# A hybrid attention and MLP layer in split float32: GpSimd's work cut into pieces of 256 columns, the MLP's norm factor moved around the MLP, one gate filled in earlier, and h of two blocks kept on chip

## The chip, the cores and the metric

The kernel runs on one core of a Trainium2 chip. A core has five engines that run side by side, each with its own queue of instructions: TensorE (PE in the profile; PEld is its loading of weights), VectorE (DVE), ScalarE (ACT), GpSimd (POOL) and SyncE (SP), whose queue issues nearly all DMA transfers here. Work tiles live in the on-chip buffer SBUF (128 partitions), matmul results in PSUM, and everything else in the chip's main memory. The metric is the time of one execution in microseconds (us). The kernel before takes 3313.28 us, the median of 3 runs between 3307.74 and 3317.84.

## The reference

One step of a one-layer streaming encoder for 2048 prompt positions and 32 sample positions, all in float32, with model width 1024. Cut to what matters:

```
a  = rmsnorm(h, g_attn);  q, k, v of both groups = a @ w_in
oa = differential attention (4 heads, two maps each);  ob = chunk-band attention (8 heads of 64)
h  = h + concat(rmsnorm(oa), rmsnorm(ob)) @ w_out
c  = rmsnorm(h, g_mlp)              # h * rsqrt(mean(h*h) + eps) * g_mlp
h  = h + square(relu(c @ w_up)) @ w_down          # 1024 -> 4096 -> 1024
h  = h + sigmoid(h @ w_ple_gate) * (p @ w_ple_proj)
y  = rmsnorm(h, g_final)
```

The new keys and values of both groups are outputs as well. What matters for the change: the norm's factor r' = rsqrt(v), with v = mean(h*h) + eps, is one number per position, and relu squared takes a positive factor out as its square, so relu((h g r') W)^2 = relu((h g) W)^2 * r'^2, with r'^2 = 1/v.

## The kernel before

**Tiling.** The 2080 positions are the moving side of the matmuls, in four blocks of 512, 512, 512 and 544 columns (`BN`); the last is worked in two parts of 272 (`SUBS`). Features lie on the 128 partitions, eight rows of 128 for the width of 1024. Blocks go in halves, (0, 1) and (2, 3).

**Split float32.** Each operand is split into a high part (rounded to the format that TensorE reads) and a low part, the remainder. `split` (L146 to L153) does it: the high part on ACT (L149) or VectorE (L151), the low part, raw minus high, at L153 on GpSimd or VectorE. `mm3` (L164 to L170) makes a product out of three matmuls: high x high (L168), low x high (L169) and high x low (L170). `wunit` (L155 to L162) brings one weight unit of 512 KB: a DMA on SP's queue into `wr` (2 buffers), ACT makes `wh`, GpSimd makes `wl` (3 buffers each), in a single instruction over 1024 columns:

```
hi = self.wp.tile([P] + shape, F32R, tag="wh", bufs=3, name="wh")
lo = self.wp.tile([P] + shape, F32R, tag="wl", bufs=3, name="wl")
self.split(hi, lo, raw, hi_eng, lo_eng)
```

Such a unit feeds 24 matmuls per block: 8 rows x 3.

**Stages, in the order of the program.** The norm and projection of blocks 0 and 1 with the tables of the attention biases; differential attention over the first pairs of query tiles, with the projections to the other group beside it; band attention; projection of blocks 2 and 3; the norm of the band group's output for blocks 0 and 1 (`onorm`, its sums at L795 on GpSimd); differential attention over the other pairs (scores at L545, L559 and L582 for the weights e, L617 for the transposes); output projection of blocks 0 and 1 (`outproj`, L819 to L846); MLP of block 0, MLP of block 1; gate and final norm of block 1; output projection of blocks 2 and 3; gate of block 0; MLP of blocks 2 and 3 together, with the final norm of block 0 inside; gates and final norms of blocks 2 and 3.

**Around the change.** `outproj` adds the residual on VectorE (L838), squares on ACT, sums the squares on GpSimd (L844) and stores h in main memory (`hS`). `colnorm2` turns the sums into the norm's factor with two matmuls of ones, three ACT and four VectorE steps, and stores it (`rS`). `cnorm` (L847 to L862) then reads h and the factor back, row by row, multiplies by factor and g_mlp on VectorE (L859), and splits the result into cH and cL; odd rows' cL go to VectorE, even ones to GpSimd. The MLP goes over 16 chunks of 256 hidden features: `mlp_up` (L895 to L915) makes ups on TensorE, relu (L914) and square (L915) and the high part on ACT, the low part ul on GpSimd; `mlp_down` (L919 to L949) of the chunk before follows, and VectorE adds its result dps to h (L949). h is loaded into one tile per block ahead of the MLP. The gate (L966 to L1015) splits h, multiplies by w_ple_gate (gps), and works out sigmoid on ACT, VectorE (L994, L1012) and GpSimd (L997, L1014). The final norm (`final`, L1017 to L1071) transposes h on TensorE (yp) and stores y.

**What sets the order.** A planner orders each engine's instructions by simulating the engines in time, with the program's order as the priority; work of a later step moves ahead where its inputs and buffers are there. Buffers of one tag are handed out in the program's order, and space in SBUF and PSUM is taken over from whatever held it before, once that has been released. So a step that comes first in the program takes its weight buffers, PSUM banks and result tiles ahead of a step that comes later. `weave` and `weave2` interleave the pieces of two program steps by hand.

## Time and profile before

| | |
|---|---|
| median of 3 runs | 3313.28 us (3307.74 to 3317.84) |
| profiled execution | 3310.69 us, span 3308.8 us |
| mean TensorE clock granted | 0.975 of full speed |
| TensorE busy | 3096.1 us (94%), 17881 matmuls |
| VectorE busy | 1669.4 us (50%), 3952 instructions |
| ScalarE busy | 1698.4 us (51%), 3717 instructions |
| GpSimd busy | 1468.8 us (44%), 1083 instructions |
| DMA | 488.93 MB, 148 GB/s on average |

The span is the profiled stretch, from the first instruction to the last; 1.9 us of the execution's time lie outside of it. Busy time is the sum over an engine's instructions; the profile's page also gives it in 40 equal slices, a digit for tenths. A group of the profile is all instructions of one line, engine and shape: its lines read "line engine operation output<-inputs shapes xcount | busy us, mean ns | idle time of the engine ahead of them, with what ended it". A wait line names the instruction that waited, what it was released by, the total in us, how many times, and the longest. A window line gives, for a stretch from A to B us, its length, the busy time of each engine with the number of its instructions, the granted TensorE clock, the share of busy DMA engines and GB/s. A timeline line gives the start in us, the duration, and in brackets how long the engine was idle before it and what released it. Matmuls overlap in the pipeline, so that a matmul's duration is longer than the distance to the next one.

### The profile page before, as it was taken

Reading aid. Unit: us, or ns where it says so; the run is one execution under the profiler, and the core shown is the slowest. Engines: PE = TensorE matmul, PEld = TensorE weight load, DVE = VectorE, ACT = ScalarE, POOL = GpSimd, SP = SyncE. Lnnn points to the kernel's source line nnn. Section 1 sums busy time; section 2 is a strip of 40 time slices with the busy share of each in tenths; the row PEclk is TensorE's granted clock in tenths of the full one; section 3 lists DMA queues with packets and bytes.
Section 4 is the critical chain, followed back from the end, with each engine's and each line's share of the span. In section 5 each row is a group of like instructions: output and inputs, shape, how many; then the busy total and the mean of one; then the engine's idle time right before and its main releaser. Section 6 shows DMA issues by size and latency. Waiting matters only on the chain. (4 is left out here: it accounts for less than half of the span.)

```text
span 3308.8 us, 50118 instructions
## 1 busy us (share of the span) xinstructions
PE 3096.1 (94%) x17881; PEld 2710.5 (82%) x17881; DVE 1669.4 (50%) x3952; ACT 1698.4 (51%) x3717; POOL 1468.8 (44%) x1083
## 2 busy tenths in 40 slices
PE   6988989999989999999899999989889999999998
PEld 6877778889977888777777877877779999999987
DVE  6117777454555545476765656656442232223335
ACT  4226666566665766666665656654442222222245
POOL 4335654432334433444544444565753333333365
PEclk9999899999999999999999999999999999999999
DMA  7488777686788654545655345347631111111123
GB/s 232 159 252 244 205 217 205 204 247 195 215 235 215 180 145 134 155 132 138 200 136 136 112 132 144 116 146 226 178 105 52 45 46 50 46 45 45 53 86 101
DMA packets 519073, 488.93 MB, mean 148 GB/s; under 512 B 37884, under 2 KB 414016, under 8 KB 518824
## 3 DMA queue, kind: packets, MB, share of 16 engines
q1 hardware_dynamic: 518824, 485.73, 50.8%
q8 instruction: 142, 2.33, 0.3%
q14 instruction: 107, 0.88, 0.1%
HBM read 379.06 MB, written 110.49 MB: 148 GB/s over the span
## 5 line engine op out<-in xcount | busy, mean ns | idle before, releaser
L153 POOL TENSOR_TENSOR wl<-wr,wh 128x1024 fp32r<-128x1024 f32 x338 | 820.0, 2427 | 1026.3 <-ACT wh L149 983.4
L949 DVE TENSOR_TENSOR h<-h,dps 128x512 f32<-128x512 f32 (+1 forms) x640 | 373.1, 585 | 584.6 <-PE dps L170 572.2
L149 ACT ACTIVATE wh<-wr 128x1024 fp32r<-128x1024 f32 x338 | 356.9, 1056 | 563.9 <-PE dps L169 278.4
L168 PE MATMUL dps<-uh,wh 128*128 128x512 f32 (+1 forms) x1280 | 459.7, 359 | 22.0 <-DVE h L949 16.7
L168 PE MATMUL ups<-cH,wh 128*128 128x512 f32 (+1 forms) x1280 | 452.0, 353 | 8.2 <-ACT relu L914 8.0
L170 PE MATMUL dps<-uh,wl 128*128 128x512 f32 (+1 forms) x1280 | 451.7, 353 | 0.0
L169 PE MATMUL ups<-cL,wh 128*128 128x512 f32 (+1 forms) x1280 | 451.5, 353 | 0.0
L169 PE MATMUL dps<-ul,wh 128*128 128x512 f32 (+1 forms) x1280 | 451.4, 353 | 0.0
L170 PE MATMUL ups<-cH,wl 128*128 128x512 f32 (+1 forms) x1280 | 451.0, 352 | 0.0
L168 PEld LDWEIGHTS dps<-uh,wh 128*128 128x128 f32 x1280 | 242.8, 190 | 57.0 <-DVE h L949 22.8
L168 PEld LDWEIGHTS ups<-cH,wh 128*128 128x128 f32 x1280 | 241.4, 189 | 40.9 <-ACT relu L914 8.6
L170 PEld LDWEIGHTS dps<-uh,wl 128*128 128x128 f32 x1280 | 241.7, 189 | 33.0
L169 PEld LDWEIGHTS ups<-cL,wh 128*128 128x128 f32 x1280 | 241.9, 189 | 31.1 <-DVE cL L153 0.4
L170 PEld LDWEIGHTS ups<-cH,wl 128*128 128x128 f32 x1280 | 241.7, 189 | 30.1
L153 POOL TENSOR_TENSOR ul<-relu,uh 128x272 fp32r<-128x272 f32 (+1 forms) x160 | 174.9, 1093 | 205.2 <-ACT uh L149 203.8
L169 PEld LDWEIGHTS dps<-ul,wh 128*128 128x128 f32 x1280 | 242.4, 189 | 26.3
L168 PE MATMUL qps<-aH,wh 128*128 128x512 f32 (+1 forms) x640 | 231.5, 362 | 6.8 <-ACT wh L149 3.4
L545 PE MATMUL s<-ka,q 128*128 128x256 f32 (+4 forms) x784 | 192.7, 348 | 40.8 <-issue 15.7
L169 PE MATMUL qps<-aL,wh 128*128 128x512 f32 (+1 forms) x640 | 229.8, 359 | 0.0
L170 PE MATMUL qps<-aH,wl 128*128 128x512 f32 (+1 forms) x640 | 229.3, 358 | 0.0
L559 ACT ACTIVATE e<-s,nm 128x512 f32<-128x512 f32 (+3 forms) x256 | 155.1, 610 | 94.7 <-DVE nm L551 70.9
L545 PEld LDWEIGHTS s<-ka,q 128*128 128x128 f32 (+1 forms) x784 | 135.7, 195 | 66.4 <-issue 27.9
(217 smaller groups left out, 7056.9 us busy)
## 6 DMA issues: line engine op xcount, KB each, us to landing
wr<-w_up SPq DMA_DIRECT2D x96, 512.0 KB, 4.2
wr<-w_down SPq DMA_DIRECT2D x96, 512.0 KB, 3.7
wr<-w_in SPq DMA_DIRECT2D x74, 512.0 KB, 5.2
q<-qS SPq DMA_DIRECT2D x256, 128.0 KB, 4.3
v<-vSa SPq DMA_DIRECT2D x64, 512.0 KB, 3.8
ka<-kS SPq DMA_DIRECT2D x32, 512.0 KB, 7.9
wr<-w_out SPq DMA_DIRECT2D x32, 512.0 KB, 5.0
wr<-w_ple_gate SPq DMA_DIRECT2D x32, 512.0 KB, 4.4
```

The lines of the kernel that those rows point to most:

```text
L149: nc.scalar.activation(hi, raw, AF.Copy)
L153: eng.tensor_tensor(lo, raw, hi.bitcast(F32), op=ALU.subtract)
L168: nc.tensor.matmul(ps, lh, rh, start=start and i == 0, stop=False)
L169: nc.tensor.matmul(ps, lh, rl, start=False, stop=False)
L170: nc.tensor.matmul(ps, ll, rh, start=False, stop=stop and i == n - 1)
L545: nc.tensor.matmul(s, q[:, m, hl, P * qi : P * qi + nr], kt[:, m, k0 : k0 + n], start=hl == 0, stop=hl == 1)
L559: nc.scalar.activation(dst, src, AF.Exp, bias=nmx, accum_out=z[:nr, m, bi : bi + 1])
L949: nc.vector.tensor_tensor(hv, hv, ps, op=ALU.add)
```

## The change

Four things change together; which products TensorE computes does not.

1. GpSimd's two-input instructions are cut into pieces of at most 256 columns (`PW = 256`, `pool_tt`): the low parts of weights (four pieces of 256 in place of one of 1024) and of activations, the sums of squares at L795 and L844, and two steps of the gate (L997, L1014).
2. The MLP's norm factor is no longer applied to its input. The input is h g_mlp, split directly out of h (`split_g`: one ACT copy with the scale g_mlp, one VectorE step for the low part). `msnorm` makes v and r = 1/v and stores both. In `mlp`, after the first chunk's `mlp_up`, GpSimd multiplies h by v, a whole block's row at a time; in the last `mlp_down`, each row, after its last addition, is multiplied by r on VectorE, or for odd rows on GpSimd where the MLP has a single block. So (h v + sum) r = h + sum / v.
3. The gate of block 0, and its final norm, come behind the MLP of block 1 and ahead of the gate of block 1, with the loading of block 2's output-projection operands woven in; they used to come behind the output projection of blocks 2 and 3. Pools for small work tiles (`wk`, `fk`) are opened once, early, and not a second time.
4. h of blocks 2 and 3 is written by their output projections directly into the tiles that the MLP uses (`hb`), and not stored and loaded again; block 2's split is made inside its output projection, block 3's behind its own. The norm of block 3 (`msnorm(3)`) moves behind the first chunk of the MLP.

```diff
 ONQ = (8, 1, 1)
+PW = 256
...
+    def pool_tt(self, out, a, b, op):
+        nc = self.nc
+        if len(out.shape) == 2:
+            n = out.shape[1]
+            m = -(-n // PW)
+            for i in range(m):
+                sl = slice(n * i // m, n * (i + 1) // m)
+                nc.gpsimd.tensor_tensor(out[:, sl], a[:, sl], b[:, sl], op=op)
+            return
+        k, n = out.shape[1:]
+        if n > PW:
+            for i in range(k):
+                self.pool_tt(out[:, i], a[:, i], b[:, i], op)
+            return
+        s = PW // n
+        for i in range(0, k, s):
+            sl = slice(i, min(i + s, k))
+            nc.gpsimd.tensor_tensor(out[:, sl], a[:, sl], b[:, sl], op=op)
+
...
             nc.vector.tensor_copy(hi, raw)
-        eng = nc.gpsimd if lo_eng == "pool" else nc.vector
-        eng.tensor_tensor(lo, raw, hi.bitcast(F32), op=ALU.subtract)
+        if lo_eng == "pool":
+            self.pool_tt(lo, raw, hi.bitcast(F32), ALU.subtract)
+        else:
+            nc.vector.tensor_tensor(lo, raw, hi.bitcast(F32), op=ALU.subtract)
...
         self.kS = self.dram([8, 2, P, KC], F32, "kS")
-        self.vS = [self.dram([KC, D], F32, "vSa"), self.dram([KC, D], F32, "vSb")]
+        self.vS = [self.dram([KC, D], F32, "vSa"), self.dram([KC, D], F32, "vSb"), self.dram([P, T], F32, "vSm")]
...
                 nc.scalar.activation(raw, raw, AF.Square)
-                nc.gpsimd.tensor_tensor(sq, sq, raw, op=ALU.add)
+                self.pool_tt(sq, sq, raw, ALU.add)
...
-    def outproj(self, b, wk, oact, ps, acc):
+    def split_g(self, k, src, n, c):
+        nc = self.nc
+        g = self.g_mlp[:, k : k + 1]
+        hi, lo = c[0][:, k, :n], c[1][:, k, :n]
+        nc.scalar.activation(hi, src, AF.Copy, scale=g)
+        nc.vector.scalar_tensor_tensor(lo, src, g, hi.bitcast(F32), op0=ALU.mult, op1=ALU.subtract)
+
+    def outproj(self, b, wk, oact, ps, acc, hfull=None, c=None):
...
             wh, wl = self.wunit(W[:, P * d : P * d + P].rearrange("(k p) c -> p k c", p=P), [8, P])
-            h = wk.tile([P, BLK], F32, tag="tmp", bufs=4, name="hd")[:, :n]
+            if hfull is None:
+                h = wk.tile([P, BLK], F32, tag="tmp", bufs=4, name="hd")[:, :n]
+            else:
+                h = hfull[:, d, :n]
...
                 nc.scalar.activation(tmp, h, AF.Square)
-                nc.gpsimd.tensor_tensor(sq, sq, tmp, op=ALU.add)
-            self.dma(self.hS[:, d, t0 : t0 + n], h)
+                self.pool_tt(sq, sq, tmp, ALU.add)
+            if hfull is None:
+                self.dma(self.hS[:, d, t0 : t0 + n], h)
+            if c is not None:
+                self.split_g(d, h, n, c)
...
-    def cnorm(self, b, wk, act, out):
-        nc = self.nc
+    def csplit(self, b, wk, act, out, hfull=None):
...
         out[b] = (cH, cL)
-        r = wk.tile([P, BLK], F32, tag="r", bufs=2, name="rl")[:, :n]
-        self.dma(r, self.rS[:, t0 : t0 + n])
         for k in range(8):
-            tmp = wk.tile([P, BLK], F32, tag="tmp", bufs=4, name="tmp")[:, :n]
-            self.dma(tmp, self.hS[:, k, t0 : t0 + n])
-            nc.vector.scalar_tensor_tensor(
-                tmp, tmp, self.g_mlp[:, k : k + 1], r, op0=ALU.mult, op1=ALU.mult
-            )
-            self.split(cH[:, k, :n], cL[:, k, :n], tmp, "act", "dve" if k % 2 else "pool")
+            if hfull is None:
+                tmp = wk.tile([P, BLK], F32, tag="tmp", bufs=4, name="tmp")[:, :n]
+                self.dma(tmp, self.hS[:, k, t0 : t0 + n])
+            else:
+                tmp = hfull[:, k, :n]
+            self.split_g(k, tmp, n, (cH, cL))
...
-    def colnorm(self, *args):
-        out = []
-        drain(self.colnorm2(*args, out))
-        return out[0]
+    def msnorm(self, sq, b, wk, ps):
+        nc = self.nc
+        n, t0 = BN[b], 512 * b
+        sh = wk.tile([P, BLK], F32R, tag="sh", bufs=1, name="msh")[:, :n]
+        sl = wk.tile([P, BLK], F32R, tag="sl", bufs=1, name="msl")[:, :n]
+        self.split(sh, sl, sq, "act", "dve")
+        r = wk.tile([P, BLK], F32, tag="r", bufs=2, name="mr")[:, :n]
+        w = wk.tile([P, BLK], F32, tag="tmp", bufs=4, name="mw")[:, :n]
+        for s0, sn in SUBS[b]:
+            ss = ps.tile([P, 512], F32, tag="mm", name="mss")[:, :sn]
+            nc.tensor.matmul(ss, self.ones, sh[:, s0 : s0 + sn], start=True, stop=False)
+            nc.tensor.matmul(ss, self.ones, sl[:, s0 : s0 + sn], start=False, stop=True)
+            v = sq[:, s0 : s0 + sn]
+            y = r[:, s0 : s0 + sn]
+            z = w[:, s0 : s0 + sn]
+            nc.scalar.activation(v, ss, AF.Copy, scale=1.0 / D, bias=EPS)
+            nc.scalar.activation(y, v, AF.Ln)
+            nc.scalar.activation(y, y, AF.Exp, scale=-1.0)
+            nc.vector.tensor_tensor(z, v, y, op=ALU.mult)
+            nc.vector.tensor_scalar(z, z, -1.0, 2.0, op0=ALU.mult, op1=ALU.add)
+            nc.vector.tensor_tensor(y, y, z, op=ALU.mult)
+        self.dma(self.vS[2][:, t0 : t0 + n], sq)
+        self.dma(self.rS[:, t0 : t0 + n], r)
...
-    def mlp_down(self, ch, nf, blocks, us, st, wk, mm):
+    def hscale(self, blocks, st, wk, src, name):
+        out = {}
+        for b in blocks:
+            out[b] = wk.tile([P, BLK], F32, tag="r", bufs=2, name=name)
+            self.dma(out[b][:, : BN[b]], src[:, 512 * b : 512 * b + BN[b]])
+        return out
+
+    def mlp_down(self, ch, nf, blocks, us, st, wk, mm, rt=None):
...
                         nc.vector.tensor_tensor(hv, hv, ps, op=ALU.add)
+                        if rt is not None:
+                            eng = nc.gpsimd if dd % 2 and len(blocks) == 1 else nc.vector
+                            eng.tensor_tensor(hv, hv, rt[b][:, s0 : s0 + sn], op=ALU.mult)
     def mlp(self, blocks, st, wk, up, mm, md):
+        nc = self.nc
...
             yield
-            if prev is not None:
+            if prev is None:
+                vt = self.hscale(blocks, st, wk, self.vS[2], "vt")
+                for d in range(8):
+                    for b in blocks:
+                        hv = st[b][0][:, d, : BN[b]]
+                        nc.gpsimd.tensor_tensor(hv, hv, vt[b][:, : BN[b]], op=ALU.mult)
+            else:
...
             prev = us
-        self.mlp_down(ch, nf, blocks, prev, st, wk, md)
+        self.mlp_down(ch, nf, blocks, prev, st, wk, md, self.hscale(blocks, st, wk, self.rS, "rt"))
...
                     nc.scalar.activation(sg, sg, AF.Ln, bias=1.0)
-                    nc.gpsimd.tensor_tensor(sg, sm, sg, op=ALU.subtract)
+                    self.pool_tt(sg, sm, sg, ALU.subtract)
...
                     hv = h[:, d, s0 : s0 + sn]
-                    nc.gpsimd.tensor_tensor(hv, hv, sg, op=ALU.add)
+                    self.pool_tt(hv, hv, sg, ALU.add)
...
             self.small = False
+            wk = opened(top, "wk", 1)
+            fk = opened(top, "fk", 1)
...
                     self.attn_a(js, pool, ps_s, ps_t, ps_o)
-            wk = opened(sq_, "wk", 1)
-            fk = opened(sq_, "fk", 1)
             self.gfin(fk)
-            acc, cn, st = {}, {}, {}
+            cn, st = {}, {}
+            acc = {b: [] for b in range(4)}
+
             def norms(b, act, ps):
-                self.colnorm(acc[b][0], b, 1.0 / D, wk, ps, "mm", self.rS)
+                self.msnorm(acc[b][0], b, wk, ps)
                 yield
-                yield from self.cnorm(b, wk, act, cn)
-
-            acc = {b: [] for b in range(4)}
+                yield from self.csplit(b, wk, act, cn)
+
...
             up = Sized(opened(top, "uh", 16, side="right"), BLK)
-            oxs = ExitStack()
-            ox = opened(oxs, "ox", 1, side="right")
-
...
                 if b == 1:
-                    drain(self.cnorm(1, wk, actq, cn))
-                    drain(self.oload(2, ox, up, oa))
-                    oxs.close()
+                    drain(self.csplit(1, wk, actq, cn))
...
                     next(m)
-                    self.colnorm(acc[1][0], 1, 1.0 / D, wk, mm, "mm", self.rS)
+                    self.msnorm(acc[1][0], 1, wk, mm)
...
                     self.dma(self.hS[:, :, 512 * b : 512 * b + 512], h)
-            drain(self.gate(1, h, uq, actq, mm))
+            with ExitStack() as x:
+                g0 = Sized(opened(x, "g0", 2, side="right"), 512, True)
+                g0h = opened(x, "g0h", 1, side="right")
+                h0 = hload(g0h, 512, 0)
+                weave(self.gate(0, h0, uq, g0, mm), self.oload(2, wk, up, oa), 1)
+                drain(self.gate(1, h, uq, actq, mm))
+                drain(self.final(0, h0, uq, fk, mm))
...
             psx.close()
-            wk = opened(top, "wk4", 1)
-            fk = opened(top, "fk4", 1)
-            self.gfin(fk)
...
             hh = opened(top, "hh", 2, side="right")
-            weave(self.outproj(2, wk, oa[2], md, acc[2]), self.oload(3, wk, act, oa), 1, 0, OW)
-            g = self.outproj(3, wk, oa[3], md, acc[3])
+            hb = {b: hh.tile([P, 8, BLK], F32, tag="h", name="h") for b in HALVES[1]}
+            g = self.oload(3, wk, act, oa)
             next(g)
-            self.colnorm(acc[2][0], 2, 1.0 / D, wk, mm, "mm", self.rS)
+            cn[2] = [act.tile([P, 8, BLK], F32R, tag="act", name=n) for n in ("cH2", "cL2")]
+            weave(self.outproj(2, wk, oa[2], md, acc[2], hb[2], cn[2]), g, 1, 0, OW)
+            g = self.outproj(3, wk, oa[3], md, acc[3], hb[3])
+            next(g)
+            self.msnorm(acc[2][0], 2, wk, mm)
             drain(g)
-            h = hload(hh, BLK, 0)
-            g = self.gate(0, h, up, act, md)
-            next(g)
-            self.colnorm(acc[3][0], 3, 1.0 / D, wk, mm, "mm", self.rS)
-            drain(g)
-            for b in HALVES[1]:
-                drain(self.cnorm(b, wk, act, cn))
-            f = self.final(0, h, up, fk, mm)
-            st = {b: (hload(hh, BLK, b),) + cn[b] for b in HALVES[1]}
+            drain(self.csplit(3, wk, act, cn, hb[3]))
+            st = {b: (hb[b],) + tuple(cn[b]) for b in HALVES[1]}
...
             next(m)
-            drain(f)
+            self.msnorm(acc[3][0], 3, wk, mm)
...
```

## The prediction

> **What bounds the kernel now.** I read the page's busy table and slices, then the stages by window, the groups by shape, what TensorE waits for, and the timeline. The page:
>
> ```profile
> PE 3096.1 (94%) x17881; PEld 2710.5 (82%) x17881; DVE 1669.4 (50%) x3952; ACT 1698.4 (51%) x3717; POOL 1468.8 (44%) x1083
> PE   6988989999989999999899999989889999999998
> POOL 4335654432334433444544444565753333333365
> ```
>
> TensorE is busy 94% of the span; nothing else passes 51%. The change leaves the matmuls as they are, so it can win only TensorE's idle time and the time of matmuls at half rate after a gap, and lose only by new idle time. The stages (projection; attention 0 and projection of blocks 2, 3; attention 1 with output projections and MLPs of blocks 0, 1; change of stage; MLP of blocks 2, 3; last gates):
>
> ```profile
> core 0: us, PE busy (x) PEld busy (x) DVE busy (x) ACT busy (x) POOL busy (x), PEclk, DMA share, GB/s
> 0.00:650.00 650.00, 567.30 (x3433) 501.05 (x3433) 358.51 (x963) 321.04 (x841) 318.32 (x273) 0.94 0.73 214
> 650.00:1350.00 700.00, 669.12 (x4030) 590.05 (x4030) 366.96 (x1175) 453.08 (x928) 252.61 (x199) 0.98 0.68 192
> 1350.00:2150.00 800.00, 752.44 (x3796) 630.57 (x3796) 514.75 (x1088) 498.27 (x1162) 371.63 (x268) 0.99 0.52 142
> 2150.00:2460.00 310.00, 275.27 (x1446) 233.18 (x1445) 169.25 (x234) 147.91 (x275) 196.85 (x119) 0.96 0.53 165
> 2460.00:3150.00 690.00, 690.00 (x4290) 626.87 (x4289) 190.09 (x367) 194.41 (x334) 230.80 (x152) 1.00 0.17 52
> 3150.00:3309.00 159.00, 141.97 (x893) 128.75 (x891) 69.80 (x129) 83.66 (x178) 98.56 (x73) 0.96 0.29 91
> ```
>
> Length less PE busy is TensorE's idle time: 82.7, 30.9, 47.6, 34.7, 0 and 17.0 us. Length times (1 - PEclk) is about the time lost to the lower clock: 39, 14, 8, 12.4, 0 and 6.4 us. The fifth stage has nothing to win.
>
> **1. The GpSimd pieces.** Groups by shape (mean ns after the comma):
>
> ```profile
> L153 POOL TENSOR_TENSOR wl<-wr,wh 128x1024 fp32r<-128x1024 f32 x338 | 820.0, 2427 | 1026.3 <-ACT wh L149 983.4 <-ACT rsy L178 11.4 <-ACT pH L624 9.7
> L153 POOL TENSOR_TENSOR vhl<-vraw,vhl 128x256 fp32r<-128x256 f32 x64 | 48.0, 750 | 92.1 <-DVE vhl L151 74.6 <-DVE stb L713 8.6 <-DVE nm L557 3.8
> L582 DVE SCALAR_TENSOR_TENSOR e<-e,c 128x256 f32<-128x256 f32 x68 | 53.0, 785 | 1.3 <-ACT e L581 1.2
> L949 DVE TENSOR_TENSOR h<-h,dps 128x512 f32<-128x512 f32 x384 | 261.9, 683 | 535.9 <-PE dps L170 534.1
> ```
>
> The biggest GpSimd group is 338 instructions of 2.43 us. What they do to VectorE is seen in the timeline (start, us, engine):
>
> ```profile
> 68.83 0.64 DVE L151 CAST vhl<-vraw 128x256 fp32r<-128x256 f32 x1
> 69.28 2.44 POOL L153 TENSOR_TENSOR wl<-wr,wh 128x1024 fp32r<-128x1024 f32 x1
> ...
> 1515.38 2.38 POOL L153 TENSOR_TENSOR wl<-wr,wh 128x1024 fp32r<-128x1024 f32 x1 [1.28 <-ACT wh L149]
> 1515.62 2.17 DVE L572 TENSOR_SCALAR c<-c,rz 128x4 f32<-128x4 f32 x1
> ```
>
> A VectorE instruction of four columns (228 ns alone) takes 2.17 us and ends at 1517.79, the GpSimd one at 1517.76. At 68.83 a cast (289 ns alone) ran until the GpSimd piece before it was over (69.32), and wl came after it. L582 at 256 columns is 476 ns where no GpSimd instruction overlaps and 1131 where one does, while h<-h,dps, one of whose inputs is in PSUM, is 682 and 683: the two exclude one another on some operands in SBUF. Summing over all VectorE instructions the time above the unhindered duration of their form gives 251 us in 238 instructions: 98, 26, 68, 51, 0 and 9 us by stage. A wait lasts until the end of the GpSimd instruction that runs; with pieces of about 0.70 us (back-to-back 256-column ones start 696 ns apart in 71 pairs) in place of 2.36 us (155 pairs), a wait should shrink to 0.3 of itself, if VectorE gets in between two pieces. Where a second GpSimd instruction was queued right behind the first, VectorE came in at the first boundary 93 times and later 6 times. So it gets in.
>
> How much of this is on TensorE's path? Its waits (total us, times, longest):
>
> ```profile
> PE rp L311 <- DVE rsy L182: 20.9, 7, 10.9
> PE dps L168 <- DVE h L949: 16.7, 14, 3.1
> PE sb L704 <- DVE stb L707: 15.7, 14, 4.4
> PE tpp L617 <- DVE e L582: 7.5, 8, 2.3
> ```
>
> VectorE ended 74.8 us of TensorE's idle time before 2150 (38.4, 16.8, 19.6 in the first three stages). All of it, with the half-clock time behind it (28), would be -103; if what it waits for is late for other reasons, 0. Removing 0.7 of the 192 us of excess in these stages is 134 us of VectorE time, more than the 74.8; the chains are long without it too, and I take 0.58 of the 74.8, **-43**, past the middle since the chains that TensorE names are where the excess sits.
>
> What the pieces cost: every further piece adds a fixed part. A weight unit goes from 2362 to 4 x 696 = 2784 ns, +0.42 us, x338 = 143; 512 columns (1255 ns) become two at 1392, +0.14; 272 (728) two of 136, +0.14 (between the 209 ns of 32 columns and the 696 of 256); 544 three, +0.27. By stage this is +35, 37, 48, 27, 38 and 16, together 200 us; with part 3 and without the cL that go to VectorE, GpSimd comes to about 1690 us, 51%. A weight unit costs GpSimd 2.78 us and TensorE 24 matmuls of 0.23 = 5.5 us with three units in flight; that cover is gone where splits of activations queue between. I cost it at 0 before 2150; it is rival D. Late next are DMA (ka<-kS 11.0 us of TensorE's waits) and issue (15.7 at L545), which stay.
>
> The Trainium skill ("SBUF — State Buffer", section "Who interferes with whom") says that VectorE and GpSimd share one port pair under an exclusive lock, held for the whole instruction, and that "Issue order, not op shape, decides who blocks". The traces agree (2.17 us for four columns). Read strictly, queued pieces would hold VectorE as long as before, which is rival B.
>
> **2. The change of stage, 2150 to 2460.** Before, gate 1 (2154 to 2229), output projections 2 and 3 (to 2339), gate 0 (to 2406), then norms of blocks 2, 3 and the MLP. TensorE idles 34.7 us there (ACT ends 19.2, VectorE 13.0 of it) and loses 12.4 to the clock, 47 together. The dearest gap is at 2413:
>
> ```profile
> 2413.32 0.30 PE L168 MATMUL ups<-cH,wh 128*128 128x272 f32 x1
> 2421.63 0.59 PE L168 MATMUL ups<-cH,wh 128*128 128x272 f32 x1 [8.01 <-ACT relu L914]
> ```
>
> After 8.0 us of idling the same matmul takes 0.59, not 0.30, until 2426; that gap and its half rate cost 10 us. It comes from norm and split of blocks 2, 3 in a row: 4 MB read back (10.5 us per block of 2 MB), 16 of L859 and 8 cL on VectorE (medians 1.03 and 1.12) and 8 cL on GpSimd. After the change block 2 is split while its output projection runs and block 3 right after it, from the tile on chip: per 128 columns one ACT copy (0.63) and one VectorE operation (0.74 at least, L859), 8 x 0.74 = 6 us for block 3. The norm's own chain (copy, Ln, Exp, three VectorE steps) leaves the path: the first up chunk doesn't need it. Removed on the SP queue: 16 stores of h, 16 loads of it, and the two r loads; added: v and r stores and loads, eight of 0.25 MB.
>
> What takes its place: gate 0 now comes first after MLP 1, ahead of gate 1, and shares its PSUM tiles, weight and result buffers in program order; its split activations need space that attention 1 still holds. TensorE leaves MLP 1 at 2152.7, the last scores are out at 2149.7, the last transposes at 2183.2, attention's last VectorE step at 2208.6. Gate 1 filled that time. Left alone with TensorE, the rest of attention (30 us to its transposes, now interleaved with gate 1) should shrink to about 10; if it doesn't, 20 more, and the -20 below is 0. Then two gates in a row: one of 512 columns has 55.2 us of matmuls and 48.7 of GpSimd, after the change 55.7, so GpSimd leads by little: I take 6 us over both, 4 for finals, 4 for block 3's split, which waits for the output projection's operands to free their buffers, 3 for part 3. 10 + 6 + 4 + 4 + 3 = 27 against 47: **-20** (ends: all of 47 kept beside the hole, +11; only the 7.5 us of waits on weights left, -40).
>
> **3. The norm factor around the MLP.** Added: 8 multiplications of h by v per block on GpSimd, unsplit, 24 x 1.255 + 8 x 1.329 = 41 us, queued behind the first up chunk and ahead of the next chunk's weight splits. For blocks 2, 3 that is 21 us in one go; a chunk takes TensorE 690 / 16 = 43 us for four units, and three units are ahead, about 22 us of cover: the 3 us above. And the last mlp_down multiplies each result by r. In single-block MLPs half goes to GpSimd, hidden (0). For blocks 2, 3 per 128 rows: VectorE 683 + 2 x 438 and the same three again from SBUF, 2.69 with 0.74 for the first, against TensorE's 2.75: no slack, and GpSimd excludes it: **+5** (0 to +12).
>
> **4. Gates 2 and 3.** Alone at the end, 115 us of matmuls, GpSimd 48.7 + 54.5 = 103 before, 118 after: it becomes the longer. **+5** (0 to +15).
>
> **Sum.** Against the profiled execution of 3310.7 (span 3308.8 and 1.9 around it; 2.6 below the median of 3313.28): -43 - 20 + 5 + 5 = -53, so 3310.7 - 53 = **3258** us.
>
> **Rivals.** B: VectorE gains nothing. For: queued pieces may pass the lock on (against: 93 to 6), and the rsqrt chains (20.9) wait on ACT too. Only -10 is left: 3301. C: the reorder opens a wide hole: gate 0 waits until attention's last store (2222) leaving TensorE idle for 60 us, 50 more than taken: 3308. For: TensorE's tiles and the planner's slots go in order; against: the last transposes are long done by then.
>
> The Trainium skill ("TensorE: Matmul & The Clock Gate", Part 1) has the rate halve after an idle window of about 3.4 us; the row at 2421 agrees (0.59 after 8.0 us), and a hole of 60 us would add by it only some 3 us.
>
> D, slower: GpSimd becomes the bound where it is busiest. In the first, fourth and last stage it is busy 49, 63 and 62%, and the pieces add 35 + 27 + 16 = 78 us there; each lo part comes 0.42 us later. It takes the whole gain from where 53 of the 78 (68%) reach TensorE; if all do: 3258 + 78 = 3336. Against it: GpSimd sat idle 1026 us ahead of the weight splits.
>
> **How the numbers follow.** My forecast 0.53, B 0.14, C 0.08, D 0.25. The likeliest's own range is 3215 (part 1 at -75, part 2 at -31) to 3300 (part 1 at -15, part 2 at -6). The range for 8 in 10 runs from 3205 to 3338, which takes in B and C and most of D. Less than 0.3% (10 us) from the median can't be told from no change; B lies at that bound (3303) and goes half to each side: faster 0.53 + 0.07 = 0.60, same 0.07 + 0.08 = 0.15, slower 0.25.
>
> **What the profile after would show.** wl as 1352 instructions of about 0.70 us and POOL near 1690 us busy; L582 at 256 columns near 500 instead of 785 ns; TensorE's idle time before 2150 at about 118 instead of 161; no gap of 8 us ahead of ups for blocks 2, 3; gate 0's first matmul some 10 us behind MLP 1's last. The forecast is wrong if VectorE's durations fall and TensorE's idle time doesn't (late for another reason), if TensorE's waits name GpSimd's wl or ul at all often (D), or if gate 0 starts 30 us or more behind MLP 1 (C).

## The result, and the profile after

The changed kernel takes 3331.1 us (median of 8 runs, 3321.6 to 3340.0) against 3313.2 us (8 runs): a ratio of 1.0058, interval 1.0038 to 1.0077. It is slower by 0.6%, where 1.7% faster was forecast. A second measurement beside the experiments gave 1.0054 (1.0037 to 1.0070). Its profiled execution took 3321.6 us (span 3319.6), 9.5 below its median, so what is read from one trace below is put beside ratios of medians.

The page of the changed kernel, busy time by engine and TensorE's and GpSimd's slices:

```profile
PE 3104.0 (94%) x17881; PEld 2706.6 (82%) x17881; DVE 1556.1 (47%) x3963; ACT 1702.0 (51%) x3717; POOL 1728.6 (52%) x2519
PE   7988999899889999999999999868899999999998
POOL 5436776332345544655744545557584334333387
```

VectorE is 113 us less busy and GpSimd 260 us more, much as forecast (1690 us; the pieces take 0.76 us on average, not 0.70). TensorE has a new low, 8 and 6, in slices 26 and 27. The stages by window show the same. Each kernel's change of stage is cut here from the last matmul of MLP 1 to the first down matmul of blocks 2 and 3, so the cuts lie elsewhere for each. Before:

```profile
1350.00:2152.00 802.00, 754.44 (x3805) 632.20 (x3805) 516.65 (x1093) 499.09 (x1163) 373.63 (x269) 0.99 0.52 142
2152.00:2441.00 289.00, 255.28 (x1333) 216.24 (x1331) 153.62 (x192) 138.49 (x243) 191.74 (x116) 0.95 0.54 168
3165.00:3309.00 144.00, 126.97 (x798) 115.00 (x797) 57.23 (x108) 76.30 (x167) 89.08 (x67) 0.96 0.31 97
```

After (the change of stage in three parts):

```profile
0.00:650.00 650.00, 584.36 (x3609) 516.84 (x3609) 326.77 (x1019) 340.35 (x894) 371.03 (x542) 0.96 0.76 225
650.00:1350.00 700.00, 663.41 (x3924) 579.55 (x3924) 331.39 (x1122) 437.30 (x888) 288.75 (x448) 0.98 0.67 190
1350.00:2133.00 783.00, 745.58 (x3733) 622.93 (x3734) 491.21 (x1080) 495.96 (x1146) 441.87 (x606) 0.98 0.50 141
2133.00:2180.00 47.00, 17.45 (x90) 14.33 (x88) 22.46 (x46) 17.88 (x43) 18.79 (x27) 0.65 0.36 120
2180.00:2320.00 140.00, 121.92 (x488) 93.09 (x489) 32.12 (x42) 60.69 (x92) 101.80 (x141) 0.97 0.27 82
2320.00:2459.00 139.00, 126.28 (x783) 113.84 (x781) 72.49 (x131) 70.53 (x140) 88.78 (x126) 0.95 0.47 152
3180.00:3320.00 140.00, 125.19 (x792) 112.93 (x792) 63.57 (x121) 76.90 (x170) 110.05 (x173) 0.95 0.31 100
```

By the end of MLP 1 the changed kernel is 19 us ahead (2133 against 2152). Then it needs 326 us where 289 were needed before, and so the lead is lost with 18 us more; from there on it gains back 7 (720.6 us for the MLP of blocks 2, 3 against 724.3, since block 0's final norm has gone out of it, and 140 for the end against 144). The loss has a place: the 47 us from 2133 to 2180, with 17.45 us of matmuls and a granted clock of 0.65. The timeline of that place:

```profile
2132.83 0.39 PE L192 MATMUL dps<-uh,wl 128*128 128x512 f32 x1
2140.57 1.12 PE L639 MATMUL tpp<-ident,e 128*128 128x128 f32 x4 [7.20 <-DVE e L604]
2166.62 0.39 PE L665 MATMUL ss<-sl,ones_r 128*128 128x32 f32 x1
2170.24 0.25 DVE L667 SCALAR_TENSOR_TENSOR os<-os,g_sub_s,rsy 128x32 f32<-128x32 f32 x1 [1.98 <-POOL rsy L204]
2170.52 0.32 SPq L145 DMA_DIRECT2D oT<-os  x1
2170.89 0.56 SPq L145 DMA_DIRECT2D h<-hS  x1
2179.38 2.19 ACT L169 ACTIVATE hH<-h 128x512 fp32r<-128x512 f32 x4 [8.14 <-DMA h<-hS]
2180.07 0.79 PE L190 MATMUL gps<-hH,wh 128*128 128x512 f32 x1 [13.05 <-ACT hH L169]
```

MLP 1 ends at 2132.8. The rest of attention, alone on TensorE, still takes until 2167, a chain of small steps over four engines. Its last step on VectorE ends at 2170.5, and its last store (oT) goes out behind that. The load of block 0's h stands right behind this store in SyncE's queue: it goes out at 2170.9, lands 8 us later, is split on ACT, and gate 0 starts at 2180.1. The load fills space that attention held, but by the addresses in the built program this space was read for the last time at 2154 (by VectorE, which reads the bias tile `ba`). So its place in the queue held the load longer than the space did. Gate 1's h had been split by 2148 and stood ready.

### The profile page after: what moved, and what is told of

Its sections match the earlier page's. It is cut to its first block, busy times and chain, and to the rows that moved or that the text cites. A ratio compares the mean times of both kernels' runs of the same rounds, so it can differ in the third digit from the quotient of the medians.

```text
span 3319.6 us, 51567 instructions
## 1 busy us (share of the span) xinstructions
PE 3104.0 (94%) x17881; PEld 2706.6 (82%) x17881; DVE 1556.1 (47%) x3963; ACT 1702.0 (51%) x3717; POOL 1728.6 (52%) x2519
## 4 chain that ended last, share of the span: by engine, by line
PE 72%; DMA 11%; DVE 7%; ACT 4%; POOL 3%; issue 2%; SPq 1%; DVEq 0%; POOLq 0%; ACTq 0%
PE ups L190 6%; PE ups L191 6%; PE ups L192 6%; PE dps L190 6%; PE dps L191 6%; PE dps L192 6%; PE qps L190 3%; PE qps L191 3%; PE qps L192 3%; PE s L567 3%; PE ob L766 2%; DMA ka<-kS 2%; PE gps L190 2%; PE gps L191 1%; SPq L145 1%
## 5 line engine op out<-in xcount | busy, mean ns | idle before, releaser
L164 POOL TENSOR_TENSOR wl<-wr,wh 128x256 fp32r<-128x256 f32 x936 | 685.7, 764 | 491.8 <-ACT wh L169 471.5
L154 POOL TENSOR_TENSOR wl<-wr,wh 128x256 fp32r<-128x256 f32 x416 | 303.1, 760 | 394.3 <-ACT wh L169 394.0
L154 POOL TENSOR_TENSOR ul<-relu,uh 128x136 fp32r<-128x136 f32 (+1 forms) x320 | 202.8, 656 | 146.5 <-ACT uh L169 145.2
L581 ACT ACTIVATE e<-s,nm 128x384 f32<-128x384 f32 (+3 forms) x256 | 155.3, 612 | 72.9 <-DVE nm L573 52.9
```

What stands on the lines that cost most here:

```text
L154: nc.gpsimd.tensor_tensor(out[:, sl], a[:, sl], b[:, sl], op=op)
L164: nc.gpsimd.tensor_tensor(out[:, sl], a[:, sl], b[:, sl], op=op)
L581: nc.scalar.activation(dst, src, AF.Exp, bias=nmx, accum_out=z[:nr, m, bi : bi + 1])
```

## The experiments

All times are medians; ratios are to the kernel before in runs on the same chip, with 95% intervals. The groups of runs were made on different chips, so two kernels are best compared by their ratios. `a_nofac`, `a_nov` and `a_mdnov` leave the MLP's norm factor, or a part of it, out of the result.

| kernel | median us | ratio (interval) |
|---|---|---|
| changed kernel | 3331.1; again 3325.8 | 1.0058 (1.0038 to 1.0077); 1.0054 (1.0037 to 1.0070) |
| b_pieces: before, pieces alone | 3269.6; again 3274.5 | 0.9892 (0.9870 to 0.9913); 0.9887 (0.9865 to 0.9908) |
| b_p512: before, pieces of 512 | 3285.3 | 0.9934 (0.9912 to 0.9957) |
| a_whole: changed, no pieces | 3347.9 | 1.0130 (1.0105 to 1.0154) |
| a_swap: changed, gate 1 first | 3307.2 | 0.9989 (0.9974 to 1.0004) |
| a_md: a_swap, gate 0 on six banks | 3295.1 | 0.9963 (0.9948 to 0.9978) |
| a_nofac: changed, no v, no r | 3309.8 | 1.0000 (0.9989 to 1.0012) |
| a_nov: changed, no v | 3307.5 | 1.0000 (0.9985 to 1.0015) |
| a_mdv: a_md, v on VectorE | 3290.4 | 0.9946 (0.9926 to 0.9966) |
| a_pad: changed, tiles moved 96 bytes | 3320.1 | 1.0028 (1.0013 to 1.0043) |
| a_mdvpad: a_mdv, tiles moved | 3282.4 | 0.9908 (0.9892 to 0.9924) |
| b_mis: b_pieces, tiles moved 32 bytes | 3283.7 | 0.9912 (0.9894 to 0.9930) |
| b_pad4: b_pieces, late tiles moved | 3274.8 | 0.9886 (0.9869 to 0.9903) |
| a_mdnov: a_md, moved, no v | 3262.6 | 0.9856 (0.9838 to 0.9873) |
| a_hyb: a_md, moved, v and r for blocks 2, 3 only | 3260.7 | 0.9850 (0.9833 to 0.9867) |

### The pieces by themselves

My theory after the first look was that the pieces help and the new order costs; the rival was D, that the pieces' own time is the loss. `b_pieces` is the kernel before with `pool_tt` and its calls, and nothing else of the change:

```diff
+PW = 256
...
+        if lo_eng == "pool":
+            self.pool_tt(lo, raw, hi.bitcast(F32), ALU.subtract)
```

> The kernel before with one edit, GpSimd's instructions cut into pieces of at most 256 columns; order, norm and stores as before. Theory P (pieces help, the reorder costs): VectorE's time above its unhindered durations falls from 251 to about 130 us, TensorE's idle time before 2150 us falls by 20 to 25, and the time is about 3290 us (ratio 0.993). Rival D (the pieces' added GpSimd time reaches TensorE): 3325 us or more, and TensorE's waits name wl and ul.

It took 3269.6 us, 1.1% less: more than expected there, and D is out. `a_whole` asks the same from the other side:

```diff
-PW = 256
+PW = 4096
```

> The changed kernel with whole GpSimd instructions instead of pieces (PW = 4096). Theory P: it loses what the pieces gain, about 3331 + 20 = 3350 us, and MLP 1 ends some 20 us later. Rival D: the slowdown was the pieces', so it comes out at 3315 us or below.

3347.9 us, a ratio of 1.0130 against 1.0058: by the ratios the pieces gain 24 us there, where they gained 36 in the kernel before, and the two agree within their intervals. What they do on VectorE, in the groups by shape, first of the kernel before with pieces:

```profile
L604 DVE SCALAR_TENSOR_TENSOR e<-e,c 128x256 f32<-128x256 f32 x68 | 44.5, 660 | 1.3 <-ACT e L603 1.2
```

and of the changed kernel, with the pieces of the weights' low parts (two lines of the helper, 936 + 416 = 1352 of them):

```profile
L164 POOL TENSOR_TENSOR wl<-wr,wh 128x256 fp32r<-128x256 f32 x936 | 685.7, 764 | 491.8 <-ACT wh L169 471.5 <-ACT rsy L200 11.3 <-PE tpb L741 6.5
L154 POOL TENSOR_TENSOR wl<-wr,wh 128x256 fp32r<-128x256 f32 x416 | 303.1, 760 | 394.3 <-ACT wh L169 394.0
L604 DVE SCALAR_TENSOR_TENSOR e<-e,c 128x256 f32<-128x256 f32 x68 | 46.8, 694 | 1.4 <-ACT e L603 1.4
```

L604 is the L582 of the kernel before, 785 ns there. It fell to 660 and 694, not to 500: VectorE's time above its unhindered durations went from 251 us in 238 instructions to 144 in 318 (136 in 309 in the changed kernel). Each wait is shorter, but there are more of them. That the wait goes with the length of the running piece was put to the test with two pieces per weight:

```diff
-PW = 256
+PW = 512
```

> The kernel before with GpSimd's instructions cut into pieces of at most 512 columns: a weight's low part in two pieces of 1.25 us instead of one of 2.36 or four of 0.70. Theory L (VectorE waits for the end of the running piece, so the gain goes with the piece's length): (2.36 - 1.25) / (2.36 - 0.70) = 0.67 of the 41 us that 256 columns gave, about 27, so 3284 us. Rival: any cut gives the whole, since VectorE only needs one boundary, and less is paid in added GpSimd time: 3270 us or less.

3285.3 us, as the length says (3284), not 3270: a shorter piece is worth its added fixed time here. TensorE's idle time up to the end of MLP 1 is 150 us in its trace, where it is 161 before and 140 with pieces of 256, so about half of that drop is there too.

### The order of the gates

`a_swap` puts gate 1 back ahead of gate 0 in the program:

```diff
                 h0 = hload(g0h, 512, 0)
+                drain(self.gate(1, h, uq, actq, mm))
                 weave(self.gate(0, h0, uq, g0, mm), self.oload(2, wk, up, oa), 1)
-                drain(self.gate(1, h, uq, actq, mm))
                 drain(self.final(0, h0, uq, fk, mm))
```

> The changed kernel with the gate of block 1 first in the program, ahead of block 0's, all else kept. Theory P: gate 1's matmuls fill the stretch in which attention ends; the hole of 47 us with 17 us of matmuls goes, about -35 us: 3296 us. Rival: the loss is not of the order but of two gates on two PSUM banks and of GpSimd in a row, then the hole moves behind gate 1 and the time is 3320 us or more.

3307.2 us: 0.69% less than the changed kernel, 23 us of the 35 expected. The window behind MLP 1's end, and TensorE's timeline there, in this kernel:

```profile
2141.00:2190.00 49.00, 42.48 (x211) 34.77 (x210) 24.51 (x45) 26.55 (x53) 36.29 (x50) 0.93 0.29 90
```

```profile
2140.60 0.39 PE L192 MATMUL dps<-uh,wl 128*128 128x512 f32 x1
2140.82 0.31 PE L567 MATMUL s<-ka,q 128*32 128x160 f32 x2
2140.97 0.43 PE L190 MATMUL gps<-hH,wh 128*128 128x512 f32 x1
```

Gate 1's first matmul follows MLP 1's last by 0.4 us, and 49 us hold 42.5 of matmuls instead of 17.5 in 47: the hole is the order's. What was still lost sat in the gates: TensorE waited there 13 us for VectorE to read gps (sm) and 8 us at one pps. Both gates run on the two PSUM banks that attention leaves, where gate 0 had six before the change. `a_md` gives attention's banks back ahead of gate 0:

```diff
                 drain(self.gate(1, h, uq, actq, mm))
+                psx.close()
+                md = opened(top, "md", 8 - MM, PSUM, "right")
-                weave(self.gate(0, h0, uq, g0, mm), self.oload(2, wk, up, oa), 1)
+                weave(self.gate(0, h0, uq, g0, md), self.oload(2, wk, up, oa), 1)
```

> The kernel with the gate of block 1 first (3307 us), and in addition block 0's gate on six PSUM banks instead of two: attention's banks are given back ahead of it. Theory B (on two banks TensorE waits for VectorE to read the gate's results; sm and sig ended 21 us of its idle time in the change of stage): about 10 us less, 3297 us. Rival: the waits are GpSimd's and ACT's chain anyway, 3305 us or more.

3295.1 us, 12 less; by the ratios it is 0.26% or 9 us, and the intervals overlap a little. Together the order and the banks cost 0.95%, 31 us, with intervals far apart. The stretch from MLP 1's end to the first down matmul is 326 us in the changed kernel's trace, 305 in that of `a_swap` and 291 in this one.

### The norm factor

`a_nofac` drops both multiplications, `a_nov` only the one by v; this is the edit of `a_nov`:

```diff
             if prev is None:
-                vt = self.hscale(blocks, st, wk, self.vS[2], "vt")
-                for d in range(8):
...
-                        nc.gpsimd.tensor_tensor(hv, hv, vt[b][:, : BN[b]], op=ALU.mult)
+                pass
```

> The changed kernel without the multiplications of h by v and of the sum by r (and their two loads); this leaves the MLP's norm factor out of the result. It prices part 3. Theory P: the multiplications lie beside other work, 3326 to 3331 us. Rival N: they hold VectorE, GpSimd or the first chunk, and the time falls by 10 us or more, to 3320 us or below.

> The changed kernel without the multiplication of h by v (and its load); the one by r stays. This leaves v out of the result. Leaving out both took 21 us off the median. Theory V: GpSimd's 8 or 16 multiplications in one go, ahead of the low parts of the next chunk in its queue, are the cost: 3331 - 18 = 3313 us. Rival R: VectorE's multiplications by r in the last down chunk are the cost: 3328 us or more.

3309.8 and 3307.5 us, both at ratio 1.0000: the factor costs 0.58%, 19 us, all of it v's; r costs nothing that can be told. That is against my theory for `a_nofac`. In the timeline of the changed kernel GpSimd shows where, behind the first chunk of MLP 0:

```profile
1073.39 0.92 POOL L154 TENSOR_TENSOR ul<-relu,uh 128x256 fp32r<-128x256 f32 x1
1075.40 10.00 POOL L1024 TENSOR_TENSOR h<-h,vt 128x512 f32<-128x512 f32 x8 [1.09 <-DMA vt<-vSm]
1085.33 1.44 POOL L154 TENSOR_TENSOR ul<-relu,uh 128x256 fp32r<-128x256 f32 x2
1086.69 1.45 POOL L154 TENSOR_TENSOR wl<-wr,wh 128x256 fp32r<-128x256 f32 x2
```

and TensorE:

```profile
1086.82 0.80 PE L191 MATMUL dps<-ul,wh 128*128 128x512 f32 x1 [3.36 <-POOL ul L154]
1087.41 0.63 PE L192 MATMUL dps<-uh,wl 128*128 128x512 f32 x1
1087.84 0.63 PE L191 MATMUL dps<-ul,wh 128*128 128x512 f32 x1
```

Eight multiplications hold GpSimd for 10.0 us. The low parts ul of the second half of the chunk, which the first down matmuls need, come behind them; TensorE idles 3.4 us and goes on at about half rate (0.63 us each, 0.43 from one to the next, where 0.39 and 0.23 are usual). Against the trace without v the changed kernel goes from 6 us ahead at the first down matmul to 5 behind twelve of them later. These twelve take 14 to 15.4 us in all five traces of kernels with pieces of 256 that multiply by v on GpSimd there (8.4 in that of `a_whole`), and 4.5 to 4.6 in those of `a_nov`, `a_nofac` and `a_mdnov`. So about 11 of the 19 us are lost here; two chunks on, 8 of them are still missing. Behind v in MLP 1 no such step is seen in the changed kernel's trace. In those of `a_md` and `a_pad` TensorE waits 8.4 and 8.7 us around there, at attention's scores; in the traces of the changed kernel and of `a_nov` it is 2.6 and 3.1. So a part of the rest may lie there, but one trace of each kernel does not settle it.

With v on VectorE:

```diff
-                        nc.gpsimd.tensor_tensor(hv, hv, vt[b][:, : BN[b]], op=ALU.mult)
+                        nc.vector.tensor_tensor(hv, hv, vt[b][:, : BN[b]], op=ALU.mult)
```

> As the kernel with six banks, and the multiplication of h by v on VectorE instead of GpSimd (0.68 us for 512 columns where GpSimd takes 1.26). Theory V: it gives back most of what the multiplication cost, about 15 us, so 3282 us. Rival: VectorE's queue pays as much as GpSimd's did, 3297 us.

3290.4 us, 0.9946 against 0.9963 with overlapping intervals: inconclusive, and not the 15 us expected. VectorE's queue is held much as GpSimd's was:

```profile
1077.16 7.68 DVE L1024 TENSOR_TENSOR h<-h,vt 128x512 f32<-128x512 f32 x7 [5.82 <-DMA vt<-vSm]
```

Behind these seven TensorE waits 5.0 us for a step of band attention on VectorE (`stb`), and the twelve down matmuls take 15 us again.

### Where the operand tiles lie

Beyond these, the trace of the changed kernel had its 512-column matmuls of the first blocks further apart. Four of MLP 1's, of the kernel before:

```profile
1736.06 0.39 PE L168 MATMUL ups<-cH,wh 128*128 128x512 f32 x1
1736.29 0.39 PE L169 MATMUL ups<-cL,wh 128*128 128x512 f32 x1
1736.52 0.39 PE L170 MATMUL ups<-cH,wl 128*128 128x512 f32 x1
1736.74 0.39 PE L168 MATMUL ups<-cH,wh 128*128 128x512 f32 x1
1736.97 0.39 PE L169 MATMUL ups<-cL,wh 128*128 128x512 f32 x1
```

and of the changed kernel:

```profile
1711.12 0.40 PE L190 MATMUL ups<-cH,wh 128*128 128x512 f32 x1
1711.36 0.39 PE L191 MATMUL ups<-cL,wh 128*128 128x512 f32 x1
1711.59 0.39 PE L192 MATMUL ups<-cH,wl 128*128 128x512 f32 x1
1711.82 0.40 PE L190 MATMUL ups<-cH,wh 128*128 128x512 f32 x1
1712.06 0.40 PE L191 MATMUL ups<-cL,wh 128*128 128x512 f32 x1
```

Four steps take 0.91 us before and 0.94 after; over all of them the median step is 227 ns and 234 ns. No engine waits. What differs is where the operands lie: the change opens `wk` and `fk` ahead of the operand tiles, and so, by the addresses in the built programs, these move from byte 50976 of each partition to byte 77504, from 32 to 192 above a multiple of 256. `a_pad` makes one tile in `fk` longer, so that they lie 32 above one again; the late tiles of blocks 2 and 3 move with them:

```diff
-        self.gf = pool.tile([P, D], F32, name="gf")
+        self.gf = pool.tile([P, D + 24], F32, name="gf")[:, :D]
```

> The changed kernel with one tile of the small-tile pool made 96 bytes longer, so that the operand tiles opened after it start at a multiple of 256 bytes plus 32, as before the change, and not plus 192. In the changed kernel's trace 512-column matmuls of the first two blocks' up and output projections start 234 ns apart, before the change 227. Theory L (the place of the moving operand sets this; opening wk and fk earlier moved it): 227 ns again, 1536 + 384 matmuls x 6.5 ns and 1536 x 3 in the down projection, 17 us less, 3314 us. Rival: it is the load of GpSimd or memory traffic, the spacing stays at 234 and the time at 3331 us.

The step was 227 ns again in the up and output projections of blocks 0, 1 (and 231 instead of 234 in the down projection), and the median 3320.1 us: 0.30%, 10 us less, not the 17 expected, and the intervals overlap a little. The other way round, `b_mis` moves the tiles of the kernel with pieces off their place:

```diff
+            pad = opened(sq_, "padq", 1).tile([P, 8], F32, name="pad")
+            self.nc.vector.memset(pad, 0.0)
             actq = Sized(opened(sq_, "actq", 2), 512, True)
```

> The kernel before with pieces of 256 columns (3270 us), and a tile of 32 bytes (set once) opened ahead of the operand tiles, so that these start at a multiple of 256 bytes plus 64 instead of plus 32. Theory L: 512-column matmuls of the first blocks' up and output projections go from 227 to 234 ns apart, and the time rises by 15 us to about 3285. Rival: no change, 3270 us.

The step went from 227 to 234 ns and the median from 3269.6 to 3283.7 us, 0.2% by the ratios, within their intervals. `b_pad4` moves the late tiles, with rows of 2176 bytes, in the same manner (`fk4`'s gf longer by 24 columns):

> The kernel before with pieces of 256 columns (3270 us), and the late operand tiles (blocks 2, 3 and the last gates, 234 ns apart before and after) moved by 96 bytes to the same place as the early ones. Their rows lie 2176 bytes apart, not 2048. Theory L: between 227 and the 231 that the first projection's tiles of that row length have, so 3 to 7 ns on about 1900 matmuls of 512 columns, 6 to 13 us less: 3257 to 3264 us. Rival: no change.

Their step fell from 234 to 232 ns, and the ratio of 0.9886 can't be told from 0.9892: no gain. Last, `a_mdv` with the longer gf:

> Gate 1 first, gate 0 on six PSUM banks, the multiplication by v on VectorE (3290 us), and the 96 bytes. Theory L: about 17 us less and what the late tiles gain, 3265 to 3273 us. Rival: 3290 us.

0.9908 against 0.9946, with intervals apart: 0.38%, 13 us. The step's length is shown in each pair. Its price in time is about 10 us here, and only this last pair is by itself beyond its intervals.

### Do the causes add up?

`a_mdnov` takes all three losses out of the changed kernel (gate 1 first, six banks, tiles moved, no v):

> The changed kernel with gate 1 first, gate 0 on six banks, the operand tiles moved by 96 bytes, and no multiplication by v (its factor is left out of the result). Theory S (the prices add up): 3331 - 36 - 10 - 24 = 3261 us, at or below the kernel before with pieces (3270). Rival: v's price was mostly other things and does not come off again; from 3282 (the same with v on VectorE) only the local 10 us, 3272 us or more.

3262.6 us, 0.9856. By the single steps 1.0058 - 0.0095 - 0.0058 - 0.0030 = 0.9875 was due: they add up, within 0.2%. `a_again` and `b_again` repeat both ends on the same chip:

> The changed kernel itself beside the others, as the upper end of the sum: ratio 1.0058, about 3331 us.

> The kernel before with pieces of 256 columns once more, beside the others: ratio 0.989, about 3270 us.

The last kernel keeps from the change what didn't cost: `a_hyb` is `a_md` with the tiles moved, the old `colnorm` and `cnorm` for blocks 0 and 1, and v and r for blocks 2 and 3.

```diff
-            if prev is None:
+            if prev is None and len(blocks) > 1:
                 vt = self.hscale(blocks, st, wk, self.vS[2], "vt")
...
-                self.msnorm(acc[b][0], b, wk, ps)
+                self.colnorm(acc[b][0], b, 1.0 / D, wk, ps, "mm", self.rS)
...
-            drain(self.csplit(1, wk, actq, cn))
+            drain(self.cnorm(1, wk, actq, cn))
```

> As that, but with the norm factor on the MLP's input, as before the change, for blocks 0 and 1, and around the MLP (v and r) for blocks 2 and 3 alone. Theory S with v's cost in the single-block MLPs: the same time as without v, 3261 to 3266 us. Rival: v costs in blocks 2 and 3 too, or the old norm costs as much in blocks 0 and 1: 3275 us or more.

3260.7 us, 0.9850 (0.9833 to 0.9867): the fastest of all, 1.5% below the kernel before and below the pieces alone (0.9887 beside it). With v kept for blocks 2, 3 it is as fast as without any, so v costs nothing there, unless the old norm of blocks 0 and 1 gained as much as v cost; no run separates the two. Its change of stage:

```profile
2113.00:2402.00 289.00, 259.50 (x1362) 220.03 (x1361) 125.51 (x218) 144.57 (x270) 207.63 (x288) 0.95 0.42 131
```

## Why the prediction was wrong

**Part 1, the pieces: -43, measured -36 (0.9890).** The mechanism and the size were right, though not the split. TensorE's idle time up to MLP 1's end fell by 21 us (161 to 140, where 118 was forecast), and what VectorE ended of it from 74.8 to 58.6 only, since more VectorE instructions meet a piece; what ACT ended rose from 36 to 46. The other 13 of the 34 us that the trace is ahead there are half-clock time, which the prediction had kept out of its value: in the first stage the clock rose from 0.94 to 0.96. One error covered the other. Rival B is out (0.9890, not the 0.997 that it forecast), and D as well: TensorE's only wait on GpSimd of over 3 us is the ul behind v.

**Part 2, the change of stage: -20, measured +31. This is the step that failed, in the sentence "Left alone with TensorE, the rest of attention ... should shrink to about 10", which set the hole ahead of gate 0 at 10 us.** The hole was 47 us. To its last transposes the rest of attention took 24 us alone (2133 to 2157), not 10, where it had taken 30 beside gate 1: TensorE is busy for 17.45 of the 47 us, so the rest of attention is bound by its own chain over four engines. And the forecast stopped at the transposes. Another 13 us went by until attention's last VectorE step (2170.5), and 10 more for the load of block 0's h, which stood behind attention's last store in SyncE's queue, and for its split. This is rival C, which had the mechanism ("gate 0 waits until attention's last store"), 60 us for the hole, and a chance of 0.08; its sign, a gate 0 that starts 30 us or more behind MLP 1, came. The 2222 that it gives for the store is the load of h in the profile before (2222.3); the store itself goes out at 2209.9 there. The objection raised against it, that the transposes are long done by then, was true, by 13 us, but named the wrong release: the load did not wait for them, but for its turn in the queue. Why the planner put it behind that store the runs do not show.

Two gates on two banks, put at 6 us, cost some 9 more by the ratios, which their intervals leave open. The gap of 8 us ahead of the up matmuls did go, but its gain did not stay: in its place TensorE waits 8 us for the operands of the output projections (`oact`, in the trace of `a_md`; 2 us before the change). Even in the fastest kernel, `a_hyb`, the stretch is 289 us long, as before the change, against 295 with the pieces alone.

**Part 3, the factor: +3 and +5, measured +19 and 0.** The cover ("three units are ahead, about 22 us") was worked out for blocks 2 and 3, where it held. For blocks 0 and 1 it was not worked out at all: there one block's chunk is half as long, and the ul that the first down matmul needs stands behind the multiplications, not the weights alone. r, which was given no slack, cost nothing.

**Part 4, the last gates: +5, measured 0 or less.** 140 us against 144: GpSimd's longer pieces did not become the bound.

**Left out: +10.** The prediction's list of what the change moves passed over the two pools opened earlier, which shift the operand tiles. It put the term at nothing without naming it. The spacing of 227 beside 234 ns between groups of the same shape was there to be seen in the trace before, though not what sets it.

The sum of what was measured, -36 + 31 + 19 + 10 = +24, stands against +18 for the whole; the difference of 6 us is what is left for h on chip and the direct split, within the uncertainty of the sum. The measured 3331 lies inside the range for 8 in 10 (3205 to 3338), close to rival D's 3336. That is luck: the range reached up there for D, and D's mechanism is out.

## What to carry to other kernels

Before a step is moved ahead as filler, read what its first instruction needs to have back, space included, when the last user of that lets go, and what stands ahead of its load in the queue that issues it; a step that was ready and is now second in program order can't fill in. Where two engines exclude one another, short instructions on the one are worth their fixed cost as long as the other is on TensorE's path: 1.1% here for 242 us more of GpSimd (1711 against 1469). A run of moved work on a side engine must be set against the next thing in that engine's queue, in each loop that it appears in, the shortest first.

## What was not expected of the hardware

The step between 512-column matmuls depends on where in SBUF the moving operand lies: 227 ns at 32 bytes above a multiple of 256 (rows 2048 bytes apart), 234 at 64 and at 192 above, undone by moving the tiles by 96 bytes (`a_pad`) and set by moving them by 32 (`b_mis`). Tiles with rows of 2176 bytes went from 234 to 232. Block 0's gate operands in the changed kernel, 224 above, stepped at 233 too, so not every odd multiple of 32 is a good place. What sets it these runs do not show.
